# Five S pairs instead of four in each linear of the second feed-forward, all with sums from memory, and their making carried on into the branch and output linears

## The chip, the cores and the metric

The kernel runs on one core of one Trainium2 chip. The metric is the device time of one execution in microseconds (us). Engines are named as in the profile: PE is TensorE (matmuls; PEld its weight loads), DVE is VectorE, ACT is ScalarE, POOL is GpSimd, and SP is the engine that issues most transfers. Transfers (DMA) bring weights from the device's memory (HBM) into on-chip tiles.

## The reference

One decoder layer on 272 rows (16 learned meta tokens and 256 tokens) of 2048 features, in float32: a feed-forward, a mixer of two branches (differential attention and a short convolution) with gates, and a second feed-forward, then a norm. Only the parts that the change touches:

```python
def swiglu_ffn(h, w_gu, w_down):              # w_gu 2048 x 11264, w_down 5632 x 2048
    gate, up = jnp.split(h @ w_gu, 2, axis=-1)
    return (jax.nn.silu(gate) * up) @ w_down
...
h = rms_norm(s, norm_ffn1); s = s + 0.5 * swiglu_ffn(h, ffn1_w_gu, ffn1_w_down)
h = rms_norm(s, norm_mix)                     # q, k, v, conv inputs from w_in; attention; convolution
z = jnp.einsum('blnw,nwd->blnd', ys, w_branch)
gates = jax.nn.sigmoid(h @ w_gate)
s = s + jnp.sum(gates * z, axis=2) @ w_out
h = rms_norm(s, norm_ffn2); s = s + 0.5 * swiglu_ffn(h, ffn2_w_gu, ffn2_w_down)
return rms_norm(s, norm_final)[:, 16:]
```

From the gates on, only the 256 token rows are needed.

## The kernel before

**Precision.** Each float32 operand is split in a high part (a cast to the faster float32r) and a low part (the rest). A product of two such operands takes three matmuls: high by high, low by high, high by low. For weights, ACT casts a tile "st" (128 x 1024, 0.5 MB) into "wh" and DVE subtracts it into "wl". There are three buffers of each.

**Stages, in order.** (1) The first feed-forward: `linear` calls (L311), each 16 chunks of 128 rows by 512 columns of weights (its down linears 24 or 20), in blocks of two chunks with 24 matmuls of 272 columns. (2) The mixer's input linears q, k, v, c, u, b, also by `linear`, with the attention's steps laid between. (3) For each half of the width: a gate linear "g", a branch linear "z", another "g", another "z", made by `Mixed`. (4) Four output linears "o" (`Plain`). (5) The second feed-forward: its 11 groups of 512 hidden features are taken in thirds of 4, 4 and 3; for each group a gate/up linear "pg", and after each third two down linears "pd" (u = 0 and 1), all by `Mixed`. The very last of these is held open for the end of the kernel and is all "D".

**D and S pairs.** A `Mixed` linear computes a 256 x 1024 output (as 2 x 2 blocks of 128 x 512) from eight pairs of chunks (six in the last third's down linears). For a "D" pair the 2 x 2 by 2 x 2 block product is done directly: 8 products, 24 matmuls of 512 columns, in two slots. For an "S" pair it is done in the Strassen-Winograd form: 7 products, 21 matmuls, in four slots (of 2, 2, 2 and 1 products). The 7 products need sums of the weight blocks, four half tiles "ta" and "tb", and sums of the activation blocks (the "b" tile of a pair).

**Sums in memory.** For some S pairs `Store` makes ta and tb ahead of time: `want` lists the units; `tick`, called by `linear` once a block (L336), loads a unit's two tiles "ur" and "un" on SP's queue at every sixth tick, and three ticks later DVE does four adds (L302 to L305, 128 x 512 each) into "ua" and "ub", which POOL's queue writes to memory. `Mixed.mixed` then reads ta and tb, and only half of the second weight tile. The third S pair of each whole linear is not in the store (`in_store`, n != 2) and gets its sums from four DVE adds in place. All of st, ur, un, ua, ub, sr, sx, ta and tb share eight buffers of tag "st". Before, there are 47 units: 3 in each of 11 gate/up linears, 3 in each of the four down linears of the whole thirds, 2 in the one of the last third.

**Order.** The tile framework orders each engine's instructions when the program is built and gives out the buffers. `stream` (L664) runs the slots: the casts and rests of a slot are prepared two slots ahead; after a slot's products come its `after` steps, and then up to `room` entries of `todo`, a list of small DVE steps (evictions, the splitting of m). A D slot has room 2, an S slot room 0. DVE instructions that go through `dve` keep their written order. `turned` (L471) transposes a group's result into the activations m of the down linear, at slots 4 and 5 of the next linear (`LATER_AT`): for a D pair one cast and one subtraction; for an S pair `combine`, three steps: first (cast and subtract, "ma"), sums (three small subtractions in "xf"), low (cast and subtract, "mb").

**Which pairs.** HALF = "DDDSSDSS" for gate/up, TURNED = "DSDSDSDS" for the down linears of whole thirds, run in ORDER (0, 2, 4, 1, 3, 6, 5, 7), that is D D D S S D S S; SHORT = "DDDSDS" for the last third. Activations lie in 28 buffers of tag "act"; an S pair takes two of them, a D pair one.

Of the kernel before, what the change touches and what calls it, by code (L numbers as in the profile page):

```python
# [9 lines left out]
F32 = mybir.dt.float32  # L10
# [5 lines left out]
P = 128  # L16
# [3 lines left out]
T = SEQ + NMETA  # L20
F = 5632
DC = D // P
GC = 4
GW = GC * P
W2 = D // 2
# [7 lines left out]
SCRATCH = 4096  # L33
N_EV = 8
ST_BUFS = 8
N_ACT = 28
EVICT_AT = 1
WARM = 6
SPARE = 3
HOLD = 3  # L40
LATER_AT = (4, 5)
MIXED = "DDDSDSDS"
HALF = "DDDSSDSS"
TURNED = "DSDSDSDS"
ORDER = (0, 2, 4, 1, 3, 6, 5, 7)
SHORT = "DDDSDS"
STEP = 6
SQUARES = {2: (0, 1), 4: (2, 3), 6: (4, 5), 8: (6, 7, 8), 10: (9, 10, 11), 12: (12,), 14: (13, 14, 15)}


# [1 line left out]
def decoder_layer(ctx: ExitStack, tc: tile.TileContext, t, out):  # L52
# [15 lines left out]
    def raw_tile(name):  # L68
        return wpool.tile([P, 2, GW], F32, tag="st", bufs=ST_BUFS, name=name)
# [34 lines left out]
        nc.tensor.matmul(warm[:, :P], ident, ident, start=True, stop=True)  # L104


    grow = const.tile([DC, P], F32, name="grow")
# [16 lines left out]
    vrows = const.tile([NV, P], F32, name="vrows")  # L124
    G_MIX, G_FFN2, G_CONV, G_SUB = 0, DC, 2 * DC, NV - 1

    def load_gain(g0, src):
# [8 lines left out]
    lamv = const.tile([P, 4, HD], F32, name="lamv")  # L136
    for i, n in enumerate(("lambda_q1", "lambda_k1", "lambda_q2", "lambda_k2")):
        nc.gpsimd.dma_start(out=lamv[:, i, :], in_=t[n][0:1, :].to_broadcast([P, HD]))

# [29 lines left out]
        nc.vector.tensor_copy(vec, vp[:, :NV])  # L169

    def make_lam():
        lprod = tmp.tile([P, 2, HD], F32, tag="lprod", bufs=1, name="lprod")
        nc.vector.tensor_mul(lprod, lamv[:, 0:4:2, :], lamv[:, 1:4:2, :])
        ldot = const.tile([P, 2], F32, name="ldot")
        nc.vector.tensor_reduce(out=ldot, in_=lprod, axis=AX.X, op=ALU.add)
        lexp = const.tile([P, 2], F32, name="lexp")
        nc.scalar.activation(lexp, ldot, AF.Exp)
        nc.vector.tensor_sub(lam, lexp[:, 0:1], lexp[:, 1:2])
        nc.vector.tensor_scalar_add(lam, lam, LAM_INIT)
        nc.vector.tensor_scalar_mul(subg, col(G_SUB), 1.0 - LAM_INIT)  # L180
# [38 lines left out]
    class Norm:  # L219
# [5 lines left out]
        def add(self, c):  # L225
            first = self.ssq is None
            if first:
                self.ssq = tmp.tile([P, T], F32, tag="ssq", name="ssq")
            sq = self.ssq if first else tmp.tile([P, T], F32, tag="sq", name="sq")
            self.act.activation(sq[:, self.n0 :], s(c, self.n0), AF.Square)  # L230
            if not first:
                self.last = self.dve.tensor_add(self.ssq[:, self.n0 :], self.ssq[:, self.n0 :], sq[:, self.n0 :])

        def end(self):
            n0 = self.n0
            ps = bank("ssq_ps")
            nc.tensor.matmul(ps[:, n0:T], ones, self.ssq[:, n0:], start=True, stop=True)
            ms = tmp.tile([P, T], F32, tag="ms", bufs=1, name="ms")
# [15 lines left out]

    def rsqrt(out_, ms, shape, name):

        a = tmp.tile([P, T], F32, tag="rsa", bufs=1, name="rsa" + name)[:, : shape[1]]
# [9 lines left out]
    class Store:  # L267
# [10 lines left out]
        def get(self, w, r0, c0):  # L278
            return self.kept.get((w.tensor.name, r0, c0))

        def tick(self):
            n = self.count % STEP
            self.count += 1
            if self.count <= 0:
                return
            if n == 0 and self.units:
                w, r0, c0, c1, _ = self.units[0]
                self.v = [raw_tile(n) for n in ("ur", "un")]
                for tl, cq in zip(self.v, (c0, c1)):
                    nc.sync.dma_start(  # L290
                        out=tl, in_=w[r0 : r0 + 2 * P, cq : cq + GW].rearrange("(c p) f -> p c f", p=P)
                    )
            if n == STEP // 2 and self.v:
                kept = self.units.pop(0)[-1]
                (r, x), self.v = self.v, None
                ta, tb = raw_tile("ua"), raw_tile("ub")
                added(nc.vector, r, x, ta, tb)
                for tl, to in zip((ta, tb), kept):
                    nc.gpsimd.dma_start(out=to, in_=tl.rearrange("p c f -> p (c f)"))

    def added(v, r, x, ta, tb):
        v.tensor_add(ta[:, 0, :], r[:, 0, :], x[:, 0, :])  # L302
        v.tensor_add(ta[:, 1, :], x[:, 1, :], x[:, 0, :])
        v.tensor_add(tb[:, 0, :], ta[:, 0, :], x[:, 1, :])
        v.tensor_add(tb[:, 1, :], tb[:, 0, :], r[:, 1, :])  # L305

    store = Store()
    pending = []
# [201 lines left out]
    class Mixed:  # L510
# [54 lines left out]
        def direct(self, g, kept):  # L565
            v = {}
            self.held = getattr(self, "held", [])

            def prep(k):
                sw = self.load(g, k)  # L570
                v[k] = new_w(kept)
                cast(v[k], sw)
                rest(v[k], sw)

            def half(k, i, q, *f):
                wh, wl = v[k]
                self.product(
                    ("C11", "C12", "C21", "D22")[2 * i + q],
                    lambda lo: self.act.part(2 * g + k, lo, i),
                    wh[:, q, :], wl[:, q, :], *f,  # L580
                )

            def products(k):
                for i in range(2):
                    if i and kept:
                        self.held.append(lambda q, *f: half(k, 1, q, *f))
                        continue
                    for q in range(2):
                        half(k, i, q)

            for k in range(2):
                self.slots.append(Slot(lambda k=k: prep(k), lambda k=k: products(k), 2))

        def mixed(self, g):
# [3 lines left out]
                self.product(n, lambda lo: self.act.block(g, x, lo), wt[0][:, q, :], wt[1][:, q, :])  # L598

            kept = store.get(self.w, (self.k0 + 2 * g) * P, self.c0)  # L600

            def raw():
                r, x = v["sr"], v["sx"] = raw_tile("sr"), raw_tile("sx")
# [36 lines left out]
            def p(*xs):  # L640
# [1 line left out]
                    part(x, n, v[key], q)  # L642

            self.slots += [
                Slot(raw, lambda: p((1, "P1", "r", 0), (2, "C11", "r", 1)), 0),
                Slot(sums, lambda: p((5, "P5", "a", 0), (4, "P7", "a", 1)), 0),
                Slot(sums2, lambda: p((6, "P6", "b", 0), (3, "C21", "b", 1)), 0),
                Slot(single, lambda: p((7, "C12", "s", 0)), 0),
            ]

        def late(self, end):
# [33 lines left out]
    class Plain:  # L685


        def __init__(self, act, w, c0, name, evict, steps=()):
# [280 lines left out]
    def in_store(kinds, order):  # L969
        at = [g for g in order if kinds[g] == "S"]  # L970
        return [g for n, g in enumerate(at) if n != 2]

    for third in thirds:
        whole = len(third) == GC
        for g in third:
            for k in in_store(HALF, range(8)):
                store.want(w_gu, 2 * k * P, g * GW, F + g * GW)
        kinds, order = (TURNED, ORDER) if whole else (SHORT, range(6))
        for u in range(2 if whole else 1):
            for k in in_store(kinds, order):  # L980
                store.want(w_down, (third[0] * GC + 2 * k) * P, u * W2, u * W2 + GW)

    before1 = First()

# [78 lines left out]
    class Unit:  # L1063
# [47 lines left out]
        def values(self):  # L1111
            h, qt, g, j = self.h, self.qt, self.g, self.j
            po = bank("po")
            nc.tensor.matmul(po[:, :P], self.aA, vA[:, h, :], start=True, stop=False)
            for i in range(qt + 1):
                nc.tensor.matmul(po[:, :P], self.aB[:, i, :], vN[g][:, i, j, :], start=False, stop=i == qt)
            nc.vector.tensor_copy(oN[g][:, qt, j, :], po[:, :P])
            junk = tmp.tile([P, P], F32, tag="junk", bufs=1, name="junk")
# [209 lines left out]
    for third in thirds:  # L1328
# [12 lines left out]
        for u in range(2):  # L1341
# [52 lines left out]
            )  # L1394
            turns = []
    stream(linears)


_INS = [
# [22 lines left out]
```

## Time and profile before

| | us |
|---|---|
| median of 3 runs | 2188.62 (2188.53 to 2189.38) |
| the profiled execution | 2188.72 |
| its span, first to last instruction | 2186.9 |

The granted TensorE clock of that execution is 0.999. The stages start, by the first matmul of each in the timeline, at about 8.6 us (first feed-forward), 815 (mixer's linears), 1130 (gates and branches), 1388 (output) and 1483 (second feed-forward). The first unit's adds are at 59.3 us, the last one's at 891.9.

```
PE   9999999999999999999999999999999999999998
DVE  7767665566766767666777787768888988888888
ACT  6434333333433444444445555556666566655665
DMA  7787888879888988744556665656777877878874
GB/s 238 263 309 275 294 295 288 301 261 317 302 276 287 320 294 303 260 145 135 167 162 212 212 207 190 211 180 216 250 239 258 280 238 259 273 244 277 282 244 154
```

This is how to read it: the span is cut in 40 slices of 54.7 us; a digit is the busy share of an engine in tenths (9 is 90% or more); DMA is the mean busy share of the 16 DMA engines, and the last row is what they moved. In rows of groups, a name such as "wl<-st,wh" says what is written from what, and "x246" how many instructions the group has.

### The profile page before, as it was taken

The numbers are of one execution on the slowest core, as the hardware profiler recorded it, in microseconds if no ns is written. First come the engines' busy times: TensorE is split into PE (matmuls) and PEld (weight loads), VectorE is DVE, ScalarE is ACT, GpSimd is POOL, SyncE is SP. The second block draws the span as 40 slices with busy tenths as digits, with TensorE's granted clock in tenths as the row PEclk, the third lists the DMA queues.
The fourth block names the chain that finished last, engine by engine and source line by source line (L and its number), as shares of the span: only waits on it lengthen the run. The fifth ranks groups of instructions, "written<-read, shape, count | busy, mean of one in ns | idle before, by whom it ended". The sixth has DMA issues, their size and how long they took to land.

```text
span 2186.9 us, 34858 instructions
## 1 busy us (share of the span) xinstructions
PE 2173.7 (99%) x13450; PEld 1955.7 (89%) x13450; DVE 1643.5 (75%) x2214; ACT 1109.3 (51%) x1431; POOL 60.6 (3%) x119
## 2 busy tenths in 40 slices
PE   9999999999999999999999999999999999999998
PEld 8999999999999999999988888888878888888886
DVE  7767665566766767666777787768888988888888
ACT  6434333333433444444445555556666566655665
POOL 0000000000000000000000000000000000000000
PEclk9999999999999999999999999999999999999999
DMA  7787888879888988744556665656777877878874
GB/s 238 263 309 275 294 295 288 301 261 317 302 276 287 320 294 303 260 145 135 167 162 212 212 207 190 211 180 216 250 239 258 280 238 259 273 244 277 282 244 154
DMA packets 240966, 542.09 MB, mean 248 GB/s; under 512 B 18564, under 2 KB 18624, under 8 KB 240800
## 3 DMA queue, kind: packets, MB, share of 16 engines
q1 hardware_dynamic: 225184, 484.25, 66.5%
q0 software_dynamic: 15232, 54.96, 6.7%
q8 instruction: 105, 1.72, 0.3%
q10 hardware_dynamic: 384, 0.66, 0.1%
q14 instruction: 61, 0.50, 0.1%
HBM read 486.18 MB, written 53.61 MB: 247 GB/s over the span
## 4 chain that ended last, share of the span: by engine, by line
PE 98%; ACT 1%; DVE 1%; DMA 1%; issue 0%; DVEq 0%
PE pgC L560 12%; PE pdC L560 7%; PE pgP L560 6%; PE gC L560 5%; PE pd L346 4%; PE pu L346 4%; PE pu L344 4%; PE pd L344 4%; PE pu L345 4%; PE pd L345 4%; PE pg L346 4%; PE pg L344 4%; PE pg L345 4%; PE zC L560 3%; PE o L709 3%; PE pgD L560 3%
## 5 line engine op out<-in xcount | busy, mean ns | idle before, releaser
L331 ACT CAST wh<-st 128x1024 fp32r<-128x1024 f32 x352 | 369.6, 1051 | 566.9 <-PE pd L345 134.8
L332 DVE TENSOR_TENSOR wl<-st,wh 128x1024 fp32r<-128x1024 f32 x352 | 429.6, 1222 | 273.8 <-ACT wh L331 273.2
L84 DVE TENSOR_TENSOR wl<-st,wh 128x1024 fp32r<-128x1024 f32 x246 | 299.3, 1220 | 85.2 <-ACT wh L504 78.2
L504 ACT CAST wh<-st 128x1024 fp32r<-128x1024 f32 x238 | 247.4, 1053 | 184.2 <-PE o L709 39.9
L344 PE MATMUL pg<-h,wh 128*128 128x272 f32 x704 | 202.8, 289 | 1.7 <-ACT wh L84 1.4
L344 PE MATMUL pu<-h,wh 128*128 128x272 f32 x704 | 203.2, 289 | 0.0
L346 PE MATMUL pd<-m,wl 128*128 128x272 f32 x704 | 203.0, 288 | 0.0
L346 PE MATMUL pu<-h,wl 128*128 128x272 f32 x704 | 203.0, 288 | 0.0
L344 PE MATMUL pd<-m,wh 128*128 128x272 f32 x704 | 203.0, 288 | 0.0
L345 PE MATMUL pu<-h,wh 128*128 128x272 f32 x704 | 202.4, 288 | 0.0
L345 PE MATMUL pd<-m,wh 128*128 128x272 f32 x704 | 202.4, 287 | 0.0
L345 PE MATMUL pg<-h,wh 128*128 128x272 f32 x704 | 201.4, 287 | 0.0
L346 PE MATMUL pg<-h,wl 128*128 128x272 f32 x704 | 199.7, 289 | 0.0
L560 PE MATMUL pgC<-wh,h 128*128 128x512 f32 x528 | 163.3, 391 | 0.0
L344 PEld LDWEIGHTS pg<-h,wh 128*128 128x128 f32 x704 | 132.3, 188 | 2.6 <-ACT wh L84 2.6
L504 ACT CAST wh<-ta 128x1024 fp32r<-128x1024 f32 x74 | 77.9, 1052 | 108.3 <-DVE ta L84 72.7
L345 PEld LDWEIGHTS pg<-h,wh 128*128 128x128 f32 x704 | 132.8, 189 | 0.0
L345 PEld LDWEIGHTS pu<-h,wh 128*128 128x128 f32 x704 | 132.7, 189 | 0.0
L345 PEld LDWEIGHTS pd<-m,wh 128*128 128x128 f32 x704 | 132.7, 189 | 0.0
L346 PEld LDWEIGHTS pu<-h,wl 128*128 128x128 f32 x704 | 132.5, 188 | 0.0
L346 PEld LDWEIGHTS pd<-m,wl 128*128 128x128 f32 x704 | 132.5, 188 | 0.0
L344 PEld LDWEIGHTS pu<-h,wh 128*128 128x128 f32 x704 | 132.2, 188 | 0.1
(479 smaller groups left out, 5162.0 us busy)
## 6 DMA issues: line engine op xcount, KB each, us to landing
st<-in_ffn_w_gu_dram SPq DMA_DIRECT2D x176, 512.0 KB, 5.9
st<-in_ffn_w_down_dram SPq DMA_DIRECT2D x140, 512.0 KB, 6.2
st<-in_w_in_dram SPq DMA_DIRECT2D x96, 512.0 KB, 4.4
st<-in_ffn_w_gu_dram SPq DMA_DIRECT2D x176, 256.0 KB, 4.3
sr<-in_ffn_w_gu_dram SPq DMA_DIRECT2D x44, 512.0 KB, 4.2
st<-in_w_gate_dram SPq DMA_DIRECT2D x40, 512.0 KB, 4.7
ur<-in_ffn_w_gu_dram SPq DMA_DIRECT2D x33, 512.0 KB, 7.8
un<-in_ffn_w_gu_dram SPq DMA_DIRECT2D x33, 512.0 KB, 5.0
```

The source lines that it names most:

```text
L84: r = f(*a, **k)
L331: act_.copy(out=wh[:, :m, :], in_=sw)
L332: dve_.tensor_sub(wl[:, :m, :], sw, wh[:, :m, :].bitcast(F32))
L344: nc.tensor.matmul(a, wh[:, i, f], act.part(c, 0, t0, t1), start=first, stop=False)
L345: nc.tensor.matmul(a, wh[:, i, f], act.part(c, 1, t0, t1), start=False, stop=False)
L346: nc.tensor.matmul(a, wl[:, i, f], act.part(c, 0, t0, t1), start=False, stop=last)
L504: nc.scalar.copy(out=wt[0][:, : sw.shape[1], :], in_=sw)
L560: nc.tensor.matmul(ps[:, f0:f1], x, wt[:, f0:f1], start=count[n] == self.whole[n], stop=count[n] == 1)
L709: nc.tensor.matmul(a, wh[:, i, f], act.both(c, 0, SEQ), start=first, stop=False)
```

## The change

The kinds of pairs become FIVE = "DDDSSSSS" for gate/up, TURNED = "DSDSDSSS" with ORDER (0, 2, 4, 1, 3, 5, 6, 7), run as D D D S S S S S, and SHORT = "DDDSSS". `in_store` goes: every S pair of the second feed-forward reads its sums from memory, 78 units in all. A unit is started at every fifth tick; its adds are done in two parts, ua at the second tick after the loads and ub at the third, each written out at once. `tick` is now also called when a slot of a branch linear ("z") or an output linear ("o") is prepared, with its DVE work in the written order of `dve`. S slots whose sums come from memory get room 1. "act" has 30 buffers; small tiles that had buffers of their own take "ev" buffers in exchange.

```diff
-N_ACT = 28
+N_ACT = 30
-HALF = "DDDSSDSS"
-TURNED = "DSDSDSDS"
-ORDER = (0, 2, 4, 1, 3, 6, 5, 7)
-SHORT = "DDDSDS"
-STEP = 6
+FIVE = "DDDSSSSS"
+TURNED = "DSDSDSSS"
+ORDER = (0, 2, 4, 1, 3, 5, 6, 7)
+SHORT = "DDDSSS"
+STEP = 5
...
-        lprod = tmp.tile([P, 2, HD], F32, tag="lprod", bufs=1, name="lprod")
+        lprod = ev([P, 2, HD], "lprod")
...
-        def tick(self):
+        def tick(self, v=nc.vector):
             n = self.count % STEP
...
-            if n == STEP // 2 and self.v:
+            if n == 2 and self.v:
+                r, x = self.v
+                ta = raw_tile("ua")
+                self.v.append(ta)
+                v.tensor_add(ta[:, 0, :], r[:, 0, :], x[:, 0, :])
+                v.tensor_add(ta[:, 1, :], x[:, 1, :], x[:, 0, :])
+                nc.gpsimd.dma_start(out=self.units[0][-1][0], in_=ta.rearrange("p c f -> p (c f)"))
+            if n == 3 and self.v:
                 kept = self.units.pop(0)[-1]
-                (r, x), self.v = self.v, None
-                ta, tb = raw_tile("ua"), raw_tile("ub")
-                added(nc.vector, r, x, ta, tb)
-                for tl, to in zip((ta, tb), kept):
-                    nc.gpsimd.dma_start(out=to, in_=tl.rearrange("p c f -> p (c f)"))
+                (r, x, ta), self.v = self.v, None
+                tb = raw_tile("ub")
+                v.tensor_add(tb[:, 0, :], ta[:, 0, :], x[:, 1, :])
+                v.tensor_add(tb[:, 1, :], tb[:, 0, :], r[:, 1, :])
+                nc.gpsimd.dma_start(out=kept[1], in_=tb.rearrange("p c f -> p (c f)"))
...
             def prep(k):
                 sw = self.load(g, k)
+                if self.name == "z":
+                    store.tick(dve)
...
             kept = store.get(self.w, (self.k0 + 2 * g) * P, self.c0)
+            room = 0 if kept is None else 1
...
-                Slot(raw, lambda: p((1, "P1", "r", 0), (2, "C11", "r", 1)), 0),
+                Slot(raw, lambda: p((1, "P1", "r", 0), (2, "C11", "r", 1)), room),
...
             def prep(b):
                 sw = raw_tile("st")
+                store.tick(dve)
                 nc.sync.dma_start(
...
-            for k in in_store(HALF, range(8)):
-                store.want(w_gu, 2 * k * P, g * GW, F + g * GW)
+            for k in range(DC // 2):
+                if FIVE[k] == "S":
+                    store.want(w_gu, 2 * k * P, g * GW, F + g * GW)
...
-    h3 = Pairs("h3", HALF)
+    h3 = Pairs("h3", FIVE)
```

More of the change, by code (lines that the diff above doesn't have):

```diff
@@ L104, in decoder_layer @@
         nc.tensor.matmul(warm[:, :P], ident, ident, start=True, stop=True)
-    grow = const.tile([DC, P], F32, name="grow")
+    grow = ev([DC, P], "grow")
     nc.scalar.dma_start(out=grow, in_=t["norm_ffn1"][0].rearrange("(c p) -> c p", p=P))
@@ L123, in decoder_layer @@
     NV = 2 * DC + 3 * NH + 1
-    vrows = const.tile([NV, P], F32, name="vrows")
+    vrows = ev([NV, P], "vrows")
     G_MIX, G_FFN2, G_CONV, G_SUB = 0, DC, 2 * DC, NV - 1
@@ L135, in decoder_layer @@
     nc.gpsimd.dma_start(out=vrows[G_SUB:NV, :], in_=t["subln"])
-    lamv = const.tile([P, 4, HD], F32, name="lamv")
+    lamv = ev([P, 4, HD], "lamv")
     for i, n in enumerate(("lambda_q1", "lambda_k1", "lambda_q2", "lambda_k2")):
@@ L227, in add @@
             if first:
-                self.ssq = tmp.tile([P, T], F32, tag="ssq", name="ssq")
-            sq = self.ssq if first else tmp.tile([P, T], F32, tag="sq", name="sq")
+                self.ssq = ev([P, T], "ssq")
+            sq = self.ssq if first else ev([P, T], "sq")
             self.act.activation(sq[:, self.n0 :], s(c, self.n0), AF.Square)
@@ L237, in end @@
             nc.tensor.matmul(ps[:, n0:T], ones, self.ssq[:, n0:], start=True, stop=True)
-            ms = tmp.tile([P, T], F32, tag="ms", bufs=1, name="ms")
+            ms = ev([P, T], "ms")
             nc.vector.tensor_scalar(ms[:, n0:], ps[:, n0:T], 1.0 / D, EPS, op0=ALU.mult, op1=ALU.add)
@@ L255, in rsqrt @@
     def rsqrt(out_, ms, shape, name):
-        a = tmp.tile([P, T], F32, tag="rsa", bufs=1, name="rsa" + name)[:, : shape[1]]
+        a = ev([P, T], "rsa" + name)[:, : shape[1]]
         nc.scalar.activation(a, ms, AF.Sqrt)
@@ L292, in tick @@
                     )
-            if n == STEP // 2 and self.v:
-                kept = self.units.pop(0)[-1]
-                (r, x), self.v = self.v, None
-                ta, tb = raw_tile("ua"), raw_tile("ub")
-                added(nc.vector, r, x, ta, tb)
-                for tl, to in zip((ta, tb), kept):
[L299 to L305, printed above, removed]
+            if n == 2 and self.v:
[6 more added lines that the diff above has]
+            if n == 3 and self.v:
+                kept = self.units.pop(0)[-1]
+                (r, x, ta), self.v = self.v, None
[3 more added lines that the diff above has]
+                nc.gpsimd.dma_start(out=kept[1], in_=tb.rearrange("p c f -> p (c f)"))
     store = Store()
@@ L644, in mixed @@
             self.slots += [
-                Slot(raw, lambda: p((1, "P1", "r", 0), (2, "C11", "r", 1)), 0),
-                Slot(sums, lambda: p((5, "P5", "a", 0), (4, "P7", "a", 1)), 0),
-                Slot(sums2, lambda: p((6, "P6", "b", 0), (3, "C21", "b", 1)), 0),
-                Slot(single, lambda: p((7, "C12", "s", 0)), 0),
+                Slot(raw, lambda: p((1, "P1", "r", 0), (2, "C11", "r", 1)), room),
+                Slot(sums, lambda: p((5, "P5", "a", 0), (4, "P7", "a", 1)), room),
+                Slot(sums2, lambda: p((6, "P6", "b", 0), (3, "C21", "b", 1)), room),
+                Slot(single, lambda: p((7, "C12", "s", 0)), room),
             ]
@@ L967, in decoder_layer @@
     thirds = [list(range(0, 4)), list(range(4, 8)), list(range(8, ng))]
-    def in_store(kinds, order):
-        at = [g for g in order if kinds[g] == "S"]
-        return [g for n, g in enumerate(at) if n != 2]
     for third in thirds:
@@ L975, in decoder_layer @@
         for g in third:
-            for k in in_store(HALF, range(8)):
-                store.want(w_gu, 2 * k * P, g * GW, F + g * GW)
+            for k in range(DC // 2):
+                if FIVE[k] == "S":
+                    store.want(w_gu, 2 * k * P, g * GW, F + g * GW)
         kinds, order = (TURNED, ORDER) if whole else (SHORT, range(6))
         for u in range(2 if whole else 1):
-            for k in in_store(kinds, order):
-                store.want(w_down, (third[0] * GC + 2 * k) * P, u * W2, u * W2 + GW)
+            for k in order:
+                if kinds[k] == "S":
+                    store.want(w_down, (third[0] * GC + 2 * k) * P, u * W2, u * W2 + GW)
     before1 = First()
@@ L1117, in values @@
             nc.vector.tensor_copy(oN[g][:, qt, j, :], po[:, :P])
-            junk = tmp.tile([P, P], F32, tag="junk", bufs=1, name="junk")
+            junk = ev([P, P], "junk")
             nc.scalar.activation(junk, oN[g][:, qt, j, :], AF.Square, accum_out=osq[:, qt, h : h + 1])
@@ L1396, in decoder_layer @@
     stream(linears)
+    assert not store.units
 _INS = [
```

## Prediction

> **What bounds the kernel now.** I read the page first: its span, its busy times and the chain that ended last.
>
> ```profile
> span 2186.9 us, 34858 instructions
> PE 2173.7 (99%) x13450; PEld 1955.7 (89%) x13450; DVE 1643.5 (75%) x2214; ACT 1109.3 (51%) x1431; POOL 60.6 (3%) x119
> PE 98%; ACT 1%; DVE 1%; DMA 1%; issue 0%; DVEq 0%
> ```
>
> The chain is TensorE's (PE) from end to end. Since a pipelined matmul makes a busy PE look fuller than it is, I looked next at what PE waited for, in the view of waits for that engine; these are all its rows.
>
> ```profile
> PE warm L104 <- POOL ident masks.py:199: 2.4, 1, 2.4
> PE pg L344 <- ACT wh L84: 1.4, 2, 1.2
> PE gC L560 <- ACT wh L504: 0.2, 1, 0.2
> PE ssq_ps L237 <- DVE ssq L84: 0.2, 1, 0.2
> ```
>
> Waits of 4.2 us in 2187, nearly all at the start. No transfer, cast or subtraction makes PE wait in the steady part; all of them are hidden, some narrowly. So a matmul less is time saved, and everything that the change adds elsewhere costs nothing until it makes PE wait. The price of a matmul is read where PE runs without a break, in the chain in order of time (start, length, count):
>
> ```profile
> 2162.07 12.24 PE pdC L560 x54
> ```
>
> 12.24 / 54 = 0.2267 us for one matmul of 512 columns. The mean duration of such a row elsewhere (0.39 us) holds the pipeline's latency and would overstate it.
>
> **What is removed.** A "D" pair takes 8 products of 3 matmuls (24, 5.44 us), an "S" pair 7 (21, 4.76 us). FIVE turns one more pair from D to S in each of the 11 gate/up linears; TURNED does it in the four down linears of the two whole thirds, SHORT in the one of the last third that is not held. 16 pairs x 3 matmuls x 0.2267 = **-10.9 us**. Transposes, evictions and the last linear stay as they are.
>
> **What VectorE (DVE) gets in the second feed-forward.** These rows are from the groups by line and shape (busy us, mean ns, idle before).
>
> ```profile
> L84 DVE TENSOR_TENSOR wl<-st,wh 128x1024 fp32r<-128x1024 f32 x246 | 299.3, 1220 | 85.2 <-ACT wh L504 78.2 <-ACT wh L84 4.2
> L84 DVE TENSOR_TENSOR wl<-sx,wh 128x512 fp32r<-128x512 f32 x74 | 50.6, 684 | 0.0
> L84 DVE TENSOR_TENSOR ta<-sr,sx 128x512 f32<-128x512 f32 x27 | 18.4, 683 | 0.0
> L302 DVE TENSOR_TENSOR ua<-ur,un 128x512 f32<-128x512 f32 x47 | 32.5, 691 | 22.3 <-DMA un<-in_ffn_w_gu_dram 11.8 <-DMA un<-in_ffn_w_down_dram 9.6
> L84 DVE TENSOR_TENSOR m<-mt_ps,m 128x512 fp32r<-128x512 f32 x12 | 8.3, 692 | 19.0 <-ACT m L487 19.0
> L84 DVE TENSOR_TENSOR ma<-xf,ma 128x512 fp32r<-128x512 f32 x10 | 6.9, 692 | 20.4 <-ACT ma L447 20.4
> L84 DVE TENSOR_TENSOR mb<-xf,mb 128x512 fp32r<-128x512 f32 x10 | 6.8, 680 | 0.0
> L84 DVE TENSOR_TENSOR xf<-xf 128x128 f32<-128x128 f32 x20 | 5.9, 293 | 0.7
> L84 DVE TENSOR_TENSOR xf<-xf 128x256 f32<-128x256 f32 x10 | 4.2, 419 | 0.0
> ```
>
> A D pair costs DVE 2 x 1.22 = 2.44 us, an S pair with sums from memory 3 x 1.22 + 0.68 = 4.34, one that makes its sums 4 x 0.68 = 2.7 more. Per whole linear the change is +1.90 - 2.7 = -0.8 us, so DVE's sum falls. But five S pairs now stand in a row, 21.7 us of DVE work in 23.8 us of PE, with no D pair between. I cost this at 0: before, two S pairs in a row run at the same ratio without a wait of PE. If the cover is gone, each us of lag is a us.
>
> What does grow is the turning of m. With "DSDSDSSS" the fourth group of a third turns two S pairs, where each turned a D and an S; "DDDSSS" does the same to the last one. That is 3 linears. Windows over single linears show what a turn costs; a linear is 180 matmuls, a turned one has 8 transposes more (PE x189, with one cut by the edge):
>
> ```profile
> core 0: us, PE busy (x) PEld busy (x) DVE busy (x) ACT busy (x) POOL busy (x), PEclk, DMA share, GB/s
> 1655.00:1665.00 10.00, 10.00 (x46) 8.29 (x45) 9.96 (x13) 5.27 (x6) 0.00 (x0) 1.00 0.94 330
> 1653.26:1695.62 42.36, 42.36 (x189) 34.11 (x188) 37.13 (x45) 26.91 (x33) 0.00 (x0) 1.00 0.76 255
> 1695.64:1736.47 40.83, 40.83 (x181) 33.68 (x180) 36.07 (x41) 23.95 (x27) 0.00 (x0) 1.00 0.78 263
> 2028.76:2070.53 41.77, 41.77 (x189) 34.30 (x188) 35.86 (x41) 26.15 (x31) 0.00 (x0) 1.00 0.78 262
> ```
>
> No turn 40.83 us; two D 41.77 (the last row, a group that turns D and D); D and S 42.36. So a D replaced by an S has cost PE 0.59 us, unseen as a wait. DVE's own price of that swap is 0.69 + 0.68 + 0.42 + 2 x 0.29 = 2.37 us against 0.69, and 2.04 us of waiting for ACT against 1.58: 2.1 us. In the D slots where this falls DVE is full (9.96 of 10 us), so I put the second S between 0.59 and 2.1 and take 1.2, above the nearest row because the room is used up: **+3.6 us** (1.8 to 6.3).
>
> **Where the sums are made.** Kept units go from 47 to 78: 31 more, each 2 loads, 2 stores and 4 adds. Of 344 ticks in the linears, every 5 instead of 6 gives 69 units there and 9 in the branch and output linears. Further windows:
>
> ```profile
> 60.00:820.00 760.00, 760.00 (x6055) 760.00 (x6055) 508.40 (x675) 305.40 (x360) 46.85 (x88) 1.00 0.85 293
> 830.00:890.00 60.00, 60.00 (x430) 57.14 (x429) 40.81 (x61) 22.37 (x25) 3.19 (x6) 1.00 0.91 312
> 1030.00:1126.00 96.00, 96.00 (x676) 87.90 (x676) 71.84 (x144) 43.29 (x71) 0.00 (x0) 1.00 0.54 163
> 1172.00:1193.00 21.00, 21.00 (x95) 17.33 (x94) 15.43 (x18) 13.04 (x14) 0.00 (x0) 1.00 0.77 257
> 1194.00:1236.00 42.00, 42.00 (x185) 34.30 (x184) 32.55 (x37) 21.77 (x24) 0.00 (x0) 1.00 0.54 175
> 1388.00:1478.00 90.00, 90.00 (x526) 78.62 (x525) 62.59 (x94) 48.02 (x72) 0.00 (x0) 1.00 0.55 178
> ```
>
> In the first feed-forward 24 matmuls of 760 / 6055 = 0.1255 us make a tick of 3.01 us, so a unit must go through in 15.06 us instead of 18.07. Nine tiles of 0.524 MB in that time are 313 GB/s; 312 were moved for 60 us without a wait of PE (second row). DVE rises from 67% by 2.76 us of adds per unit to about 70%. Cost 0, hidden behind PE; that the loop of a unit is short enough is the third rival. The mixer's linears, bare of this work before (0.54 share), get it too: DVE goes from 75% to some 93% in the fourth row's stretch (2.76 / 15 added). Cost 0 by the room left; up to 3 us if DVE's bursts of evictions there fall on an add that waits. Branch linears (257 GB/s, DVE 73%) take one or two units each, output linears (178 GB/s, 70%) the rest: 0. Units that are open when a branch linear ends hold two or three of the eight "st" buffers through a gate linear; at 175 GB/s that stage needs few: 0, at most some 3 us.
>
> The moves of small tiles into "ev", two more "act" tiles for the two more halves of S pairs, and the fifth S pair of h3 (built beside the output linears, DVE 70%) are 0: PE waits on none of it today.
>
> **Sum** against the profiled execution (2188.72 us, 1.8 over its span; the median, 2188.62, is 0.1 lower): 2188.7 - 10.9 + 3.6 = **2181.4 us**.
>
> **The rivals.** *First, nothing is lost:* PE's order of matmuls hides the S and S turns; waits of 4.2 us speak for it, the 0.59 us against. With the 15 pairs gone that made their sums in place, a little of the turned linears' loss may even return. 2177.8, from 2176 to 2179.5.
>
> *Second, DVE is late in every turned linear.* The last step of an S turn (mb, 0.68 us) used to stand in the D slots between the S pairs, where DVE had room; now S slots take one such step each and it falls at the start of the run of five, where the weight splits come just in time. 10 linears x 0.68 = 6.8, and the S and S turns at 2.1 each, 6.3: 2188.7 - 10.9 + 13.1 = 2190.9, no measurable change (2184 to 2193). For it: the full DVE of the 1655 row. Against it: the run's own 2 us of room.
>
> *Third, slower: the making of sums can't keep 15.06 us.* Its chain is a loop when the next unit's second load gets the buffer that the last sums are written from. The timelines of DVE, POOL and SP, then the issues' landings, then the group of the adds:
>
> ```profile
> 152.65 0.69 DVE L305 TENSOR_TENSOR ub<-ub,ur 128x512 f32<-128x512 f32 x1
> 153.64 0.53 POOL L299 DMA_DIRECT2D sums5b<-ub  x1 [2.60 <-DVE ub L305]
> 159.99 0.37 SPq L290 DMA_DIRECT2D un<-in_ffn_w_gu_dram  x1
> sums5b<-ub POOLq DMA_DIRECT2D x1, 512.0 KB, 6.3
> un<-in_ffn_w_gu_dram SPq DMA_DIRECT2D x33, 512.0 KB, 5.0
> 206.76 0.69 DVE L302 TENSOR_TENSOR ua<-ur,un 128x512 f32<-128x512 f32 x1 [0.67 <-DMA un<-in_ffn_w_gu_dram]
> 221.87 0.69 DVE L302 TENSOR_TENSOR ua<-ur,un 128x512 f32<-128x512 f32 x1 [0.67 <-DMA un<-in_ffn_w_gu_dram]
> ```
>
> The load is issued just when the write has landed (153.64 + 6.3). From the end of the last add: 0.3 to the issue, 6.3 the write, 5.0 the load, two adds 1.3, a weight split 1.2, two adds 1.4: 15.5 us. Above 15.06 it decides: then an add waits for its load in DVE's order, the splits behind it come late, and PE waits once their lead is used. 69 units x 0.44 = 30 us at the full price: 2212; half of it, where half the units close the loop, 2197. Against it: two units did run 15.1 us apart (206.76, 221.87), and DVE can wait over 3 us a unit without harm.
>
> *Fourth, slower: transfers fall short in the run of five.* Five pairs read 5 x 3.5 tiles, 9.2 MB, in 23.8 us: 385 GB/s. The best stretch reached this:
>
> ```profile
> 2110.00:2120.00 10.00, 10.00 (x44) 8.00 (x44) 9.44 (x12) 6.88 (x9) 0.00 (x0) 1.00 1.02 390
> ```
>
> 390 would do. If 312 at a share of 0.91 (343 at 1) is what lasts, a run takes 26.7 us, 2.9 too many; with nothing fetched ahead that is 15 x 2.9 = 44 us, 2225. But eight buffers (4.2 MB) fill in the D pairs (1.05 MB in 5.44 us, 193 GB/s), which covers a shortfall of 1.0 MB; it needs a run entered with under 2.9 us in hand. [...]
>
> **How the numbers follow.** The forecast (2179.5 to 2184) has a chance of 0.40, the first rival 0.17, the second 0.20, the third 0.15, the fourth 0.05; 0.03 for what I don't see. The range goes from 2176.5, nearly all of the first rival, to 2200, which takes in the third where half its units close the loop. 0.2% is 4.4 us, about what a measurement can tell: under 2184.2 faster 0.57, same 0.22, slower 0.21.
>
> **What would show it.** Matmuls at L560's place fall by 48; their pitch stays at 0.227. Linears without a turn shrink by 0.68 us to 40.1, those with D and S to 41.7, and the three with S and S show about 1.2 more than that. Units follow each other 15 us apart and end in the output linears. If the first feed-forward's linears grow beyond 24.1 us, or rows of DVE waiting for "un" grow from 21 us to over 150, the third rival holds; casts of ta and tb that wait for a DMA show the fourth. If gate linears lengthen, the held buffers cost more than I say. A PE waiting for DVE in every linear would prove me wrong about the cover.

## The result, and the profile after

The changed kernel takes 2270.89 us (median of 4 runs, 2268.76 to 2273.88) against 2188.86 (4 runs, 2188.53 to 2189.38): a ratio of 1.0376, 95% interval 1.0358 to 1.0394. It is 82 us slower; 2181.4 was forecast, and no more than 2200. The profiled execution of after took 2273.88 us, 85.2 more than that of before.

From the page of after: its span, its busy times, and the group of the first add of a unit (busy, mean ns, idle before it and what ended that).

```profile
span 2272.1 us, 35371 instructions
PE 2197.7 (97%) x13402; PEld 1963.2 (86%) x13402; DVE 1703.8 (75%) x2325; ACT 1144.8 (50%) x1474; POOL 93.6 (4%) x181
L297 DVE TENSOR_TENSOR ua<-ur,un 128x512 f32<-128x512 f32 x69 | 47.7, 692 | 265.1 <-DMA un<-in_ffn_w_gu_dram 158.3
```

The 48 matmuls did go (13450 to 13402), and 69 units have their adds in the linears, as counted beforehand. But DVE stood 265 us in front of the first adds. The stages one by one, from first matmul to first matmul, show where the time went: first before, then after, in the order first feed-forward, mixer's linears, gates and branches, output, second feed-forward.

```profile
core 0: us, PE busy (x) PEld busy (x) DVE busy (x) ACT busy (x) POOL busy (x), PEclk, DMA share, GB/s
8.60:815.42 806.82, 805.10 (x6376) 800.71 (x6377) 547.04 (x744) 335.47 (x410) 46.32 (x87) 1.00 0.84 288
815.42:1129.98 314.56, 314.56 (x2276) 291.42 (x2275) 218.74 (x404) 145.74 (x266) 5.85 (x11) 1.00 0.62 200
1129.98:1388.52 258.54, 258.26 (x1139) 211.44 (x1137) 203.09 (x232) 138.96 (x156) 2.12 (x4) 1.00 0.62 206
1388.52:1483.33 94.81, 94.81 (x554) 82.84 (x552) 64.97 (x97) 49.89 (x74) 0.00 (x0) 1.00 0.55 179
1483.33:2145.59 662.26, 662.14 (x2940) 537.53 (x2939) 575.51 (x683) 417.57 (x493) 1.05 (x2) 1.00 0.76 256
```

```profile
9.69:861.24 851.55, 820.59 (x6378) 811.20 (x6376) 554.74 (x772) 335.61 (x409) 54.83 (x103) 0.99 0.86 293
861.24:1202.10 340.86, 323.19 (x2277) 296.81 (x2276) 252.39 (x463) 145.13 (x266) 20.74 (x39) 0.97 0.78 266
1202.10:1473.88 271.78, 263.02 (x1138) 211.56 (x1136) 214.50 (x254) 138.33 (x154) 8.49 (x16) 0.99 0.70 239
1473.88:1572.67 98.79, 95.95 (x552) 82.38 (x553) 75.61 (x114) 52.28 (x79) 3.19 (x6) 1.00 0.76 258
1572.67:2230.44 657.77, 654.82 (x2893) 528.32 (x2891) 571.73 (x668) 451.25 (x531) 1.07 (x2) 1.00 0.84 292
```

The stage that the change wants to shorten is shorter, by 4.5 us. Every stage in which the sums are made is longer: first feed-forward +44.7, mixer +26.3, gates and branches +13.3, output +4.0; the start and the last linear add 1.4. That is the 85.2. PE's busy time in the first feed-forward went up by 15.5 us for the same matmuls, and the granted clock down to 0.99 (in the mixer 0.97): part of the loss is PE standing still, part is PE running slower.

What PE waited for (us in total, times, longest), the first rows of the view of waits:

```profile
PE pd L347 <- DVE wl L333: 14.2, 8, 3.2
PE pg L347 <- DVE wl L333: 11.3, 8, 3.4
PE aT L1104 <- DVE sc L1096: 7.9, 4, 4.1
PE q L347 <- DVE wl L333: 5.2, 2, 4.6
PE pu L347 <- DVE wl L333: 4.8, 5, 1.8
```

All rows of this view sum to 64.7 us, against 4.2 before. PE waits for weight splits "wl", not for weights; and the splits are late since DVE, in its fixed order, stands at an add that waits for the transfer "un":

```profile
DVE ua L297 <- DMA un<-in_ffn_w_gu_dram: 158.3, 40, 7.8
DVE ua L297 <- DMA un<-in_ffn_w_down_dram: 85.8, 18, 6.9
```

244 us, where before had 21. Why "un" is late is seen in the timeline of one unit of after (start, length; "SPq" is an issue on SP's queue; the idle time before in brackets):

```profile
361.91 0.69 DVE L305 TENSOR_TENSOR ub<-ub,ur 128x512 f32<-128x512 f32 x1
362.89 0.41 SPq L290 DMA_DIRECT2D ur<-in_ffn_w_down_dram  x1
363.77 0.37 SPq L290 DMA_DIRECT2D un<-in_ffn_w_down_dram  x1
373.23 0.69 DVE L297 TENSOR_TENSOR ua<-ur,un 128x512 f32<-128x512 f32 x1 [6.05 <-DMA un<-in_ffn_w_down_dram]
373.84 0.69 DVE L298 TENSOR_TENSOR ua<-un 128x512 f32<-128x512 f32 x1
374.44 2.35 DVE L333 TENSOR_TENSOR wl<-st,wh 128x1024 fp32r<-128x1024 f32 x2
376.83 0.69 DVE L304 TENSOR_TENSOR ub<-ua,un 128x512 f32<-128x512 f32 x1
377.56 0.69 DVE L305 TENSOR_TENSOR ub<-ub,ur 128x512 f32<-128x512 f32 x1
378.54 0.41 SPq L290 DMA_DIRECT2D ur<-in_ffn_w_down_dram  x1
```

The two loads of a unit are issued 0.3 and 1.2 us after the last add of the unit before it. They land 9 us later, the adds and two splits between them take 5 us, and then the next pair of loads is issued: 15.65 us from one "ur" to the next, and 15.7 in the median of this stage. The ticks ask for 15.06. So the eight "st" buffers close a loop that is 0.6 us too long, and each unit is later than the one before, until PE itself stands still and lets the ticks fall back.

### The profile page after: what moved, and what is told of

Same layout as the page of the kernel before. It is cut to its first block, busy times and chain, and to the rows that moved or that the text cites. A ratio compares the mean times of both kernels' runs of the same rounds, so it can differ in the third digit from the quotient of the medians.

```text
span 2272.1 us, 35371 instructions
## 1 busy us (share of the span) xinstructions
PE 2197.7 (97%) x13402; PEld 1963.2 (86%) x13402; DVE 1703.8 (75%) x2325; ACT 1144.8 (50%) x1474; POOL 93.6 (4%) x181
## 4 chain that ended last, share of the span: by engine, by line
issue 62%; PE 32%; POOL 4%; DMA 1%; DVE 1%; ACT 1%; POOLq 0%; DVEq 0%; ACTq 0%; SPq 0%
PE pgC L561 11%; PE pgP L561 6%; PE pdC L561 6%; PE pdP L561 3%; PE pgD L561 2%; PE o L714 2%; PE pdD L561 1%; PE o L715 1%; PE mt_ps L479 0%; DVE wl L84 0%; ACT wh L505 0%; DMA sx<-in_ffn_w_gu_dram 0%; DMA sums76a<-ua 0%; DMA st<-in_w_out_dram 0%; DVE sT L84 0%
## 5 line engine op out<-in xcount | busy, mean ns | idle before, releaser
L332 ACT CAST wh<-st 128x1024 fp32r<-128x1024 f32 x352 | 368.8, 1050 | 565.1 <-PE pd L346 147.5
L333 DVE TENSOR_TENSOR wl<-st,wh 128x1024 fp32r<-128x1024 f32 x352 | 425.0, 1219 | 88.8 <-ACT wh L332 88.5
L84 DVE TENSOR_TENSOR wl<-st,wh 128x1024 fp32r<-128x1024 f32 x214 | 260.3, 1220 | 75.6 <-ACT wh L505 67.7
L505 ACT CAST wh<-st 128x1024 fp32r<-128x1024 f32 x206 | 215.0, 1052 | 157.7 <-PE pgD L561 28.6
L297 DVE TENSOR_TENSOR ua<-ur,un 128x512 f32<-128x512 f32 x69 | 47.7, 692 | 265.1 <-DMA un<-in_ffn_w_gu_dram 158.3
L345 PE MATMUL pd<-m,wh 128*128 128x272 f32 x704 | 205.7, 292 | 0.0
L346 PE MATMUL pd<-m,wh 128*128 128x272 f32 x704 | 204.9, 291 | 0.0
L347 PEld LDWEIGHTS pd<-m,wl 128*128 128x128 f32 x704 | 135.2, 192 | 16.6 <-DVE wl L333 16.4
L347 PEld LDWEIGHTS pg<-h,wl 128*128 128x128 f32 x704 | 132.4, 190 | 14.1 <-DVE wl L333 13.7
L346 PEld LDWEIGHTS pd<-m,wh 128*128 128x128 f32 x704 | 135.6, 193 | 0.0
L345 PEld LDWEIGHTS pd<-m,wh 128*128 128x128 f32 x704 | 135.2, 192 | 0.0
L346 PEld LDWEIGHTS pu<-h,wh 128*128 128x128 f32 x704 | 132.8, 189 | 0.0
```

Source lines behind the costliest of these rows:

```text
L84: r = f(*a, **k)
L332: act_.copy(out=wh[:, :m, :], in_=sw)
L333: dve_.tensor_sub(wl[:, :m, :], sw, wh[:, :m, :].bitcast(F32))
L345: nc.tensor.matmul(a, wh[:, i, f], act.part(c, 0, t0, t1), start=first, stop=False)
L346: nc.tensor.matmul(a, wh[:, i, f], act.part(c, 1, t0, t1), start=False, stop=False)
L347: nc.tensor.matmul(a, wl[:, i, f], act.part(c, 0, t0, t1), start=False, stop=last)
```

## The experiments

The theory after the first look: **buffers**, as just told. Its rivals: **bandwidth** (a unit every 15 us is more than the memory can deliver), **the place of the adds** (at the second tick they stand too early in DVE's order, whatever the buffers), and **the kinds** (the run of five S pairs costs in some other way). Times are medians; each ratio is to the kernel before, run on the same chip (2188.77 to 2189.19 us), with its 95% interval.

### The pace, and with it the place of the adds

```diff
-STEP = 6
+STEP = 5
```

> The kernel before with STEP 5 instead of 6 and nothing else: 47 units, the same kinds of pairs, four adds at the second tick. If the pace of the units is what costs (a unit's round of loads, adds and writes through the eight st buffers takes about 16 us, and five ticks are 15.1), the first feed-forward grows by 0.9 us a unit, 30 to 45 us, and the time is 2218 to 2234. If the new kinds of pairs or the ticks in branch and output linears cost it, this stays at 2189.

Measured: 2245.19 us, ratio 1.0257 (1.0237 to 1.0278). This is the kernel before with one number changed, and the same 47 units, all of them made in the first feed-forward. The number does two things: units start every five ticks, and since the adds stand at tick `STEP // 2`, they move from the third tick to the second. The window of the first feed-forward:

```profile
8.62:869.62 861.00, 823.72 (x6375) 812.22 (x6376) 552.07 (x764) 334.66 (x410) 51.63 (x97) 0.99 0.83 284
```

All other stages are as before (second feed-forward 662.9). So this one number costs 56 us, more than I expected, and all of it in the stage that I had costed at 0. The view of DVE's waits:

```profile
DVE ua L302 <- DMA un<-in_ffn_w_gu_dram: 131.4, 31, 7.8
DVE ua L302 <- DMA un<-in_ffn_w_down_dram: 62.4, 13, 6.5
```

Here the loop is the one that the prediction drew. The timelines of POOL and SP of this kernel, at one unit:

```profile
351.68 0.53 POOL L299 DMA_DIRECT2D sums18b<-ub  x1 [2.06 <-DVE ub L305]
352.55 0.40 SPq L290 DMA_DIRECT2D ur<-in_ffn_w_gu_dram  x1
358.72 0.37 SPq L290 DMA_DIRECT2D un<-in_ffn_w_gu_dram  x1
```

"un" is issued 7.0 us after the write of the sums, just when that has landed (at 358.70); 30 of the 47 units wait for such a write. Over the whole stage "un" comes 5.4 us after "ur" (median). In after the two loads come 0.3 and 1.4 us behind the last add (medians), but then "un" takes 8.3 us instead of 5. Two loops through different buffers of the same eight, each about 16 us long.

### The pace, with the adds one tick later

```diff
-            if n == STEP // 2 and self.v:
+            if n == 3 and self.v:
```

> The same with the four adds at the third tick after the loads, where they stood before. If the loss comes from the adds standing one tick too early in VectorE's order, VectorE's wait for un falls by 3 us a unit and the time goes back to 2189 to 2195. If the round through the buffers is too long, later adds only free the buffers later: 2218 to 2240, like STEP 5 alone.

Measured: 2200.33 us, 1.0051 (1.0035 to 1.0067); first feed-forward 816.7, DVE's waits for "un" 95 us. The place of the adds matters more than the buffers' theory allowed: with another tick of time before DVE comes to the add, the same lateness is hidden for most units. That theory had expected 2218 or more here, and missed. The one tick also hands the buffers out in another order ("un" comes 0.4 us after "ur" again, and units follow each other at 14.9 us in the median). So this run doesn't separate the two.

### The same pace, loads in other buffers

```diff
-                self.v = [raw_tile(n) for n in ("ur", "un")]
+                self.v = [apool.tile([P, 2, GW], F32, tag="act", name=n) for n in ("ur", "un")]
```

> The kernel before with STEP 5 and ur and un in act buffers, nothing else: it differs from STEP 5 alone (2245) in the buffers of the loads only, with the same transfers at the same pace and the adds at the second tick. If the loads come late because the eight st buffers are taken, the first feed-forward is back at 806 and the time at 2186 to 2190. If early adds cost by themselves, or the transfers' rate does, it stays over 2200.

Measured: 2188.27 us, 0.9998 (0.9988 to 1.0009). This is step5_only with its loads in "act" buffers, which are idle in these stages: same pace, same adds at the second tick, same bytes. The first feed-forward is as long as before; its window, and the largest row that is left of DVE's waits for "un":

```profile
8.60:815.36 806.76, 805.06 (x6375) 800.71 (x6376) 556.40 (x764) 335.02 (x410) 51.62 (x97) 1.00 0.87 303
DVE ua L302 <- DMA un<-in_ffn_w_down_dram: 6.0, 2, 3.4
```

All waits for "un" together go from 194 us to 9, and the time falls by 57 us, by where the loads land alone. That settles the first stage: **the buffers close the loop**; the adds' early place only makes lateness visible to PE.

### The change with its loads in "act"

```diff
-                self.v = [raw_tile(n) for n in ("ur", "un")]
+                self.v = [
+                    apool.tile([P, 2, GW], F32, tag="act", name=n) if self.count < LOADS_IN_ACT else raw_tile(n)
+                    for n in ("ur", "un")
+                ]
```

LOADS_IN_ACT is 248 in the first kernel, which covers the first feed-forward, and 344 in the second, which covers all of the linears.

> The changed kernel with ur and un in buffers of tag act instead of st for the units loaded in the first feed-forward (ticks below 248); transfers, adds and pace are the same. If the shared st buffers make the units late, the first feed-forward goes from 851.5 back to about 807 and the time falls to about 2228, with the mixer, branch and output parts as slow as in the changed kernel. If the memory's bandwidth (313 GB/s asked for) or the place of the adds is the cause, the first feed-forward stays at 845 to 855 and the time at 2265 to 2275.

> The changed kernel with ur and un in act buffers for all units of the linears (ticks below 344), so in the mixer's linears too. If the mixer's 26 us more are the same late loads, the mixer goes from 334 to 340 down to about 317 and the time to about 2204 (2222 for loads in act in the first feed-forward alone). If it is VectorE's added work beside the attention, the mixer stays at 330 or more.

Measured: 2221.89 us, 1.0151 (1.0131 to 1.0171), and 2209.51, 1.0094 (1.0073 to 1.0114). With 248 the first feed-forward is back at 805.7 us; with 344 the mixer is too, but for its first linear (319.9 against 314.6). The windows of the steady part, first after, then act_loads, speak to bandwidth:

```profile
60.00:800.00 740.00, 711.76 (x5555) 705.97 (x5554) 473.36 (x638) 274.23 (x310) 49.47 (x93) 0.99 0.87 296
60.00:800.00 740.00, 740.00 (x5896) 740.00 (x5895) 511.63 (x688) 297.17 (x343) 53.18 (x100) 1.00 0.89 314
```

314 GB/s for 740 us, and PE busy in every one of them. The bytes were never the limit: the slow kernel moves fewer per second. SP's waits show who frees a buffer for the loads of weights (L325, L326, L330). One of them is a unit's third add, for which a load stands in SP's queue with everything behind it. The rows of before, after and act_loads:

```profile
SPq L325 <- DVE ub L304: 186.4, 46, 8.5
```

```profile
SPq L326 <- DVE ub L304: 139.1, 56, 5.4
```

```profile
SPq L330 <- DVE ub L308: 36.3, 13, 7.7
```

Before had that wait too, for nearly every unit; with 18.07 us a unit there was time for it. The writes of the sums hold up the same loads, each in a row of its own: in the first feed-forward 263 us in 59 waits in after, and 244 us in 66 in act_loads, where they cost nothing. Nothing on the page of before told a harmful wait from a harmless one but the sum of the loop against the new period.

### The change with its adds one tick later

```diff
-            if n == 2 and self.v:
+            if n == 3 and self.v:
...
-            if n == 3 and self.v:
+            if n == 4 and self.v:
```

> The changed kernel with ua added at the third tick after the loads and ub at the fourth (second and third in the changed kernel). STEP 5 alone cost 56 us with the adds at the second tick and 11 with them at the third, so the place of the adds carries most: if that holds here, the first feed-forward goes from 851.5 to 815 to 825, VectorE's wait for un from 244 us to about 100, and the time to 2215 to 2235. If longer holding of the eight buffers outweighs it, the first feed-forward stays over 840.

Measured: 2238.97 us, 1.0228 (1.0206 to 1.0251). The first feed-forward falls to 818.4, as expected, while waits for "un" are still 145 us. The total came out a little above what I expected, since gates and branches rise to 276.0 us and the output linears to 102.6. Units hold their buffers one tick longer there, which would explain it, but no run shows that by itself. A later add hides the loop; it doesn't open it.

### The kinds without the making

```diff
-STEP = 5
+STEP = 6
...
-                if FIVE[k] == "S":
-                    store.want(w_gu, 2 * k * P, g * GW, F + g * GW)
+            for k in (3, 4, 6, 7):
+                store.want(w_gu, 2 * k * P, g * GW, F + g * GW)
```

Both parts of the adds are at the third tick, the ticks in "z" and "o" are gone, and of the down linears' S pairs 1, 5 and 7 (4 in the last third) are kept; 57 units, and 21 pairs make their sums in place.

> The changed kernel with the old pace of the units (STEP 6, four adds at the third tick, no ticks in branch and output linears). 57 units fit, so 21 of the 78 S pairs make their sums in place. If the making alone costs, the first feed-forward is 807 as before, the second keeps most of the 10.9 us that 48 matmuls are worth (or gives a few back to VectorE's in-place sums), and the time is 2178 to 2186; the mixer's linears, which now carry units to their end, may add up to 5. If five S pairs in a row cost more than they save, the second feed-forward is 665 or longer and the time 2190 or more.

Measured: 2238.19 us, 1.0230 (1.0213 to 1.0247), far from the 2178 to 2186 expected. The stages before the second feed-forward are as before (805.7, 315.5, 258.3, 94.8), but that takes 708.2 us against 657.8 in after. The loss is 50 / 21 = 2.4 us for each pair whose sums are made in place, which is also the length of its four adds, 0.60 us from one to the next. Of the 50 us, 28 are PE's waits beyond those of after, and the granted clock of this stage was 0.99, in after 1.00; so the match with the adds may be chance. The largest rows of the waits:

```profile
PE pgP L560 <- ACT wh L504: 16.1, 13, 1.6
PE pdP L560 <- ACT wh L504: 10.7, 9, 1.6
```

Products of S slots wait for casts, and the casts for the sums. In the D D D S S D S S of before such a pair costs next to nothing, as the runs further down show; in a run of five it costs these 2.4 us. So the run of five does need its sums from memory, as the change has it.

### What the branch and output linears pay

```diff
-                if self.name == "z":
-                    store.tick(dve)
...
-                if kinds[k] == "S":
+                if kinds[k] == "S" and (k != 3 or whole and not u):
```

This is the kernel with LOADS_IN_ACT = 344, without the ticks in "z" and with 75 units (three pairs in place); those in "o" stay.

> As act_loads344, without ticks in the branch linears and with three pairs fewer in the store (they make their sums in place in linears that have no turn before them). If the ticks in the branch linears cost the 13 us of that part by holding st buffers, gates and branches go back from 271 to about 258.5, and the time falls 10 to 13 us under act_loads344; with the mixer healed too it is 2188 to 2194. If the branch part's loss is VectorE's or the last units' in the output linears, it stays.

Measured: 2209.38 us, 1.0095 (1.0078 to 1.0112), no better than with the ticks in "z" (2209.51). Gates and branches are back at 258.4 us, but now six units are made in the output linears, whose window shows 14.0 us more than before:

```profile
1394.05:1502.89 108.84, 100.81 (x554) 84.55 (x553) 80.27 (x124) 50.65 (x78) 6.41 (x12) 0.97 0.79 267
```

That is 2.3 us a unit; in after the nine units of "z" and "o" cost 17.3 us, 1.9 each. The three pairs in place add 5 us more in the second feed-forward: 2.2 and 2.7 us for the two in whole thirds, 0.2 for the last, against the same linears of act_loads344. It isn't the lateness of adds: between 1202 and 1573 us of after no add waits for its load. There ACT waits for weights, for which the same view of before has no row:

```profile
ACT wh L505 <- DMA st<-in_w_gate_dram: 12.2, 8, 6.4
ACT wh L505 <- DMA st<-in_w_out_dram: 10.3, 6, 6.4
ACT wh L505 <- DMA st<-in_w_branch_dram: 10.1, 9, 3.8
```

That the weights are late since open units hold their buffers is likely, but was not tried apart from the adds in DVE's order: in both kernels the loads of these stages still use "st".

### Two versions without the ticks in "z" and "o"

Both have FIVE = "DDDSSDSS" (the gate/up linears as before), the down linears with five, all sums from memory, and the loads in "act" up to near the end of the first feed-forward. From there on the first goes back to a unit every six ticks with "st" buffers, its SHORT is "DDDSDS", 66 units; the second keeps five ticks, takes "act" again in the mixer (all but ticks 240 to 255), and keeps SHORT = "DDDSSS", 67 units.

```diff
-            n = self.count % STEP
+            n = self.count % STEP if self.count < 250 else (self.count - 250) % 6
```

> Only as many kept pairs as can be made without a loss: STEP 5 with loads into act buffers in the first feed-forward, STEP 6 with st buffers and adds at the third tick in the mixer, no ticks after it: 66 units. The gate/up linears keep four S pairs, now all from memory, the down linears of the whole thirds take five, SHORT stays. 12 matmuls fewer than before (2.7 us) and no in-place adds (15 pairs at 2.4 us of VectorE). If the making is free at this pace, all parts but the second feed-forward are as before (within 2 us) and the time is 2180 to 2186, faster than both kernels. If the second feed-forward gains nothing from VectorE's relief, it is 2186; if the mixer stalls, more.

> The same with STEP 5 throughout, loads into act buffers except around the end of the first feed-forward (ticks 240 to 255), where act is full, and SHORT with three S pairs: 67 units, 15 matmuls fewer than before. If act buffers alone heal the mixer too, 2180 to 2185; if the mixer's pace of 15 us a unit costs VectorE there, its part is 317 to 325 and the time 2184 to 2192.

Measured: 2190.27 us, 1.0005 (0.9996 to 1.0014), and 2197.46, 1.0038 (1.0026 to 1.0051). In the first the making of 66 units is free: 805.8, 314.6, 258.4 and 94.8 us in the four stages. But the second feed-forward stays at 663.2: taking four sums in place out of each gate/up linear gains nothing, and 12 matmuls less in four down linears give at most 2.7 us, which is lost again there. The second loses 5.8 us in the mixer, 4.2 of them in its first linear; which part of its making does that was not tried apart.

### Five S pairs in the gate/up linears alone

The making of best66, with other pairs:

```diff
-FIVE = "DDDSSDSS"
-TURNED = "DSDSDSSS"
-ORDER = (0, 2, 4, 1, 3, 5, 6, 7)
+FIVE = "DDDSSSSS"
+TURNED = "DSDSDSDS"
+ORDER = (0, 2, 4, 1, 3, 6, 5, 7)
...
-            for k in order:
+            for k in ((3, 7) if u else (1, 3, 7)) if whole else (5,):
```

> The making of best66 (66 units, all in the linears, free there), with five S pairs in the 11 gate/up linears, all from memory (55 units), and the old kinds in the down linears, with 11 units for them: one in-place pair in each down linear with u = 0 of a whole third as before, two in those with u = 1 (no turn before them, so VectorE has room), one in the short one. 33 matmuls fewer than before, 7.5 us. The gate/up linears of the changed kernel were 5.4 us shorter in sum than before. If the S and S turns and the runs of five in the down linears are what ate the rest, the second feed-forward falls by 4 to 6 us and the time is 2182 to 2186. If in-place pairs cost 2.4 us each where they stand now, 2188 to 2193.

Measured: 2184.80 us (11 runs, 2183.66 to 2186.28), 0.9981 (0.9972 to 0.9990). It is faster than both kernels, than the one before by 4 us, which is 0.2%. The second feed-forward alone:

```profile
1483.29:2142.10 658.81, 658.13 (x2907) 531.98 (x2906) 575.63 (x673) 439.40 (x515) 1.06 (x2) 1.00 0.79 279
```

33 matmuls less are 7.5 us; 3.5 of them arrive. The other four stages stay within 2.1 us of before (804.7, 315.6, 258.3, 94.8).

## Why the prediction was wrong

**What failed is the step "Where the sums are made", and in it "Cost 0, hidden behind PE".** It rested on bytes (313 GB/s asked, 312 seen) and on DVE's share (70%). Both were right, and neither was the limit. The limit was the time for which a unit holds buffers against its new period: 0.6 us too much, measured at 45 us in the first feed-forward. With the loads in other buffers (act_loads) these 45 us are gone.

**The third rival named that mechanism, and I gave it 0.15.** It had the loop at 15.5 us against 15.06 and its test was right: the waits for "un" passed 150 us, and the linears passed 24.1. Its loop through the sums' write is the one of step5_only (about 16 us); the one of after runs through both loads. Three things in it were wrong. The 6.3 us for the write of the sums came from a single row: the 47 such writes of before took 5.2 to 10.3 us, 7.4 in the median, and with that the loop is 16.6 us, well over 15.06. The evidence against it (two units that ran 15.1 us apart) was taken at the old pace, where each unit had 18.07 us and could catch up; in both, "un" was issued 0.5 us behind "ur" and not after a write. And 30 us at the full price was 0.44 us for each of the 69 units of the linears, the mixer's included; the 51 of the first feed-forward alone lost 0.9 us each, 10 of the 45 us by the clock (an estimate: half of the 20 us that six of the stretches below last), and the branch and output linears were left out.

**The mixer, 0 to 3 us, measured 26.3.** It was judged by DVE's room (the 75% are those of the third row, 1030 to 1126), but the adds that waited for late loads took that. With the loads in "act" 21 of the 26 go; of the other 5, 4.7 are in the mixer's first linear, for a reason that stays open.

**Branch and output linears, 0, measured 14.6.** They were judged by DVE's room and the memory's rate, not by the two to four of eight buffers that an open unit takes. That these buffers are the cause fits the late weights above, but isn't shown. The gate linears, with 0 to 3 us for held buffers, were judged rightly: one of four lengthened, by 2.7.

**The clock had no term.** Half speed in 11 stretches, 41 us in all, cost an estimated 20 us (below). With the removed matmuls, 85.2 + 10.9 = 96 us were lost: 60 in PE's waits, 20 by the clock, and some 15 that show in neither.

**The second feed-forward was right in its mechanism, -4.5 for -7.3.** The matmuls are 48 fewer, their pitch stays at 0.227, and casts wait for a transfer of sums only four times, 1.6 us in all: the fourth rival falls, with 292 GB/s over the whole stage. The windows of two linears of after, one that turns two S pairs and one that turns nothing (forecast 42.9 and 40.1):

```profile
1740.29:1783.18 42.89, 42.21 (x187) 33.52 (x185) 38.62 (x47) 30.32 (x37) 0.00 (x0) 1.00 0.81 288
1783.18:1823.40 40.22, 40.22 (x179) 32.98 (x177) 35.07 (x39) 25.59 (x29) 0.00 (x0) 1.00 0.90 315
```

Summed over matmul distances, the three S and S turns cost 2.5 us more than before (1.2, 0.5, 0.8; forecast 3.6). What I had not priced are 2.8 us in linears that turn nothing, 1.9 of them in one, and 1.1 in the others: the run of five isn't quite free. DVE's work there was priced by the length of its rows, 1.22 and 0.68 us; back to back one starts 1.14 and 0.60 us after the other (medians of before; 1.13 and 0.60 in the timeline of the unit above), so a run of five takes about 20 us of DVE, not 21.7.

## What to carry to other kernels

When hidden work is to come more often, compare the time for which one round of it holds its buffers, from the first issue to the last release, with the new period; bandwidth and an engine's share of busy time don't show that limit. Work that waits for a transfer and stands in the order of an engine that also feeds the bottleneck can turn its lateness into a stall (here 244 us of waiting adds came with 60 us of waits on PE), so either give its loads buffers of their own or place it well behind their landing. And set the price of the helper against its gain in the place where it runs: here a unit cost nothing in the first feed-forward, once its loads had other buffers, but 1.9 to 2.3 us in the branch and output linears, and earned 0.68 at most.

## What the runs showed of the hardware

**In after, the granted clock was halved at the 11 longest stalls of PE.** Four stretches in a row around one stall: before it, the stall, and what follows (the third number from the end is the granted clock; "x18" counts matmuls).

```profile
320.00:324.00 4.00, 4.00 (x34) 4.00 (x33) 0.00 (x0) 1.05 (x1) 0.00 (x0) 1.00 0.75 253
324.20:327.10 2.90, 0.28 (x3) 0.06 (x1) 2.33 (x3) 0.98 (x1) 0.53 (x1) 1.00 0.69 261
327.90:331.30 3.40, 3.40 (x18) 3.40 (x17) 2.96 (x4) 0.00 (x0) 0.53 (x1) 0.51 0.94 280
331.30:334.70 3.40, 3.40 (x29) 3.40 (x29) 1.23 (x1) 1.05 (x1) 0.00 (x0) 0.99 0.92 280
```

After a stall of 2.8 us PE ran 3.4 us at a granted clock of 0.51, 18 matmuls where the next 3.4 us, at 0.99, have 29. In the body of after this happened 11 times, each time at one of the 11 longest idle times of PE (2.0 to 4.6 us), never at a shorter one (the longest, 1.8). Ten of these stretches are 3.4 us long and begin between 0.5 us ahead of the stall's end and 1.4 us behind it; the one at the stall of 4.1 us began 2.9 us ahead of its end and lasted 6.8 us. That is 41 us in all, some 3 of them within the stalls; half of the 41 is the estimate of 20 us above. In kinds57 the second feed-forward ran at 0.99, though no wait of PE in it was longer than 1.6 us; so the length of a single stall isn't all that counts, and what else does was not shown.

**A load that was issued right behind another one landed later.** In the first feed-forward of before, "un" took 8.6 us in the median of the 11 units where it was issued less than 1 us behind "ur" (7.2 to 12.3), and 4.5 in the 25 where more than 3 us lay between (3.8 to 5.9). The same shows between kernels, again in medians of this stage: 5.0 us where it was issued 5.4 us behind "ur" (step5_only), 8.1 where 0.4 us lay between (step5_add3) and 8.3 where it was 0.8 (after); the pages, with the gate/up weights of the whole kernel, have 4.6, 7.9 and 7.9. Of the 4.6 us by which "un" follows "ur" sooner in after than in step5_only, 3.3 went in its landing.
